# A hybrid decoder trunk on one core: transposes and bonus sums moved from TensorE to VectorE and DRAM trips

## Chip, core, metric

One core of a Trainium2 chip (trn2). The metric is the device time of one launch in microseconds, as the median of runs; lower is better. Matmuls run on TensorE, elementwise work on VectorE, ScalarE and GpSimd, and the DMA queues of SyncE (SP), ScalarE and GpSimd move data between DRAM and the on-chip memory.

## What is computed

Two pre-norm residual layers over 512 positions of width 1024. In each, one projection of the normed input feeds three branches, an RWKV-7 recurrence, a chunked retention and a chunked spatial gating unit; they are merged by sigmoid gates, and a gated MLP with a short causal convolution follows. The parts that the change touches, cut from the reference:

```python
def rwkv7_branch(p, mu, w0, w_up, a0, a_up, g_up, k_k, k_a, r_k, lnx_g, lnx_b):
    ...
    r, k, v, decay, a, kk = map(heads, (r, k, v, decay, a, kk))     # 8 heads of 64
    y = rwkv7_scan(r, decay, k, v, kk, a)
    mean = jnp.mean(y, axis=-1, keepdims=True)
    var = jnp.mean(jnp.square(y - mean), axis=-1, keepdims=True)
    y = (y - mean) * lax.rsqrt(var + RW_GN_EPS) * lnx_g + lnx_b
    y = y + jnp.sum(r * k * r_k, axis=-1, keepdims=True) * v        # the bonus
    return (y.reshape(B, S, RW_WIDTH) * g).astype(p.dtype)

def retention_branch(p, cos, sin):                                   # 4 heads, chunks of 128
    q, k, v, g = jnp.split(p, ...)
    q = rotary(q, cos, sin); k = rotary(k, cos, sin) * (RET_QK_DIM ** -0.5)
    scores = jnp.einsum('bhnid,bhnjd->bhnij', qc, kc) * decay_in[:, None]
    inner = jnp.einsum('bhnij,bhnje->bhnie', scores, vc)
    ...
```

## The kernel before

Every float32 matrix is split into a rounded high part and the remainder (`split`, `part`), and a product is three matmuls (`mm3`, L151): high by low, high by high, low by high. A weight unit is 128 x 512, loaded by SP (`load`, L121), split by ScalarE (L134) and VectorE (L135), and used by 12 matmuls of 512 columns. `unit` keeps three raw units and two to five split ones ahead.

A scheduler orders each engine's instructions by a modelled timeline and by the order in which the program emits them; `keep_in_program_order` (`po`) holds single instructions to the emitted order, and `pin` does so for matmuls. Engines work through their queues in that order. Tile pools have a fixed number of buffers: `u` has 31 (`NU`), `r` (pool `rg`) has 16 (`NR`), `f` 39 (`NFP`); a tile that finds none free waits for the last user of another.

A layer runs in this order.

- `rwkv`: columns of the projection give k, r, v with features on the partitions (`col`, four tiles of 128 features each, in `kc`, `rc`, `Vf`). `prep(m)` makes decays and the small products per chunk of 64 positions. `bonus(m)` multiplies r, k and `r_k` (L556), splits the product, sums it over each head's 64 partitions by two matmuls with a block matrix of ones (`bonesR`, L559 and L560) and multiplies by v (L561). It reads v as `col` left it.
- Turns by DRAM: `vturn` and `bturn` transpose 32 x 32 blocks on VectorE, write the tile to DRAM (`trip`, L229) and read it back with blocks exchanged (`turn`, L592), all on SP's queue. Four `vturn` and four `bturn(m, 0)`, the b, k of chunks 0 to 3, are emitted ahead of the solve.
- `solve`: a triangular solve of 32 x 32 blocks, a chain of some 70 VectorE instructions (L747 to L761), then `FILL[0]` filler steps and two sets of small matmuls (z at L771 into `zs`, then L780).
- The recurrence: eight chunks, each with three short bursts of 64 x 64 matmuls (L632), with one filler step ahead of each burst. In it the returned b, k are copied to their place by ScalarE (L635 before the loop, L647 inside), the state `S` is updated by VectorE (L677 to L680), and after each odd chunk y of 128 positions is normed.
- Filler steps (`fillers`) are independent projections of 12 matmuls a step: 24 gate columns, then q, k, v, g of the retention (`ret_proj`), then two of the gating unit. Inside `ret_proj`, `rotate` applies the rotary tables, fetched by ScalarE's queue (L825) when chunks 0 and 2 come up. `FILL` is (solve, between the solve's two products, recurrence). What is left of the filler runs after the recurrence.
- The rest: `sgu_v` alternates with `rwkv_out`, which transposes the four y tiles on TensorE (L712), applies scale and bias while it leaves PSUM (L714), adds the bonus and multiplies by the gate. Then merges, `ret_heads` (16 TensorE transposes of q, k at L847, copied out at L849), retention rows, output projection, and the MLP.

Of the kernel before, what the change touches and what calls it, by code (L numbers as in the profile page):

```python
# [18 lines left out]
NC = 4  # L19
# [3 lines left out]
NU, NR, NFP = 31, 16, 39  # L23
FILL = (36, 2, 1)
SEQ = "0 H 0 S 0 U S U S 0 S 0 0 S 2 2 Y 0 0 2 1 2 1 2 1 2 1 2 1 2 1 1 1"
# [22 lines left out]
class Emit:  # L48
# [170 lines left out]

    def turned(self, o, T, t):  # L220

        self.nc.vector.transpose(T.rearrange("p (f j d) -> p j f d", j=4, d=32), t.rearrange("p (j f d) -> p j f d", j=4, d=32))
        d = self.trip(T)
        for f in range(4):
            self.nc.sync.dma_start(o[32 * f:32 * f + 32, :].rearrange("d (a x) -> d a x", a=4), d[:, f * 128:f * 128 + 128].rearrange("(a d) x -> d a x", d=32))

    def trip(self, t):
        d = self.dp.tile([128, 512], F32, name=self.nm("tr"))
        self.nc.sync.dma_start(d, t)  # L229
        return d  # L230
# [69 lines left out]
    def run(self):  # L300
        nc, tc, a, V = self.nc, self.tc, self.a, self.nc.vector
        self.con = self.cp.tile([128, NCC], F32, name="con")
        self.rst = self.cp.tile([128, 512], F32, name="rst")
        self.bonesR = self.cp.tile([128, 128], F32R, name="bonesR")
        self.ones = self.cp.tile([128, 128], F32R, name="ones")
# [49 lines left out]
    def mixer(self, l, nst):  # L355
        self.pool = None
        with self.tc.tile_pool(name=f"rw{l}", bufs=1) as rp:
            self.rwp = rp
            self.filler = self.fillers(l)
            st = self.rwkv(l, nst)  # L360
        for _ in self.filler:
            pass
        self.rp = self.tc.tile_pool(name=f"ff{l}", bufs=NFP)
        self.fp = self.rp.__enter__()
        self.gup, self.bs, self.ws = self.f(n="gup"), self.f((128, 4, 128), n="bs"), self.f((128, 4, 128), n="ws")
        with self.tc.high_priority():
# [12 lines left out]
        rows = iter([(None, 0, (0, 1)), (0, 1), (1, 2, (2,)), (2, 3, (3,)), (3, None)])  # L379
        for step in SEQ.split():  # L380
            if step == "S":
                ysg += self.ret_row(*next(rows))
            elif step == "H":
                self.ret_heads()
            elif step == "U":
                next(rest), next(rest)
            elif step == "Y":
                yret = self.ret_out()
            elif step == "0":
                mg.append(self.merge(l, 0, len(mg), yrw))  # L390
# [41 lines left out]
    def rwkv(self, l, nst):  # L432
# [56 lines left out]
        X, Y, BK, Vf, bv = [], [], [], [], []  # L489
        kc, rc = [], []  # L490

        def cols3(m):
            kc.append(col(4 + m))
            rc.append(col(m))
            Vf.append(col(8 + m))

        def prep(m):


            k, r, v = kc[m], rc[m], Vf[m]  # L500
            ms = slice(m * 128, m * 128 + 128)
# [52 lines left out]
        def bonus(m):  # L554
            kp, r, v = kc[m], rc[m], Vf[m]
            V.scalar_tensor_tensor(kp, r, self.p("rk", m), kp, op0=MUL, op1=MUL)  # L556
            kh, kl = self.split(kp, self.r)
            pbn = self.sm()
            po(T.matmul(pbn, self.bonesR, kl, start=True, stop=False))  # L559
            po(T.matmul(pbn, self.bonesR, kh, start=False, stop=True))  # L560
            V.tensor_tensor(kp, v, pbn, op=MUL)  # L561
            bv.append(kp)

        if l == 0:
            self.tc.keep_in_program_order(V.memset(self.rst[:, 0:512:64], 0.0))
            A.copy(self.bonesR, self.c("bones"))
        cols3(0)
# [26 lines left out]
        def vturn(m):  # L594
            t, o = self.r(n="vT"), self.r(n="Vt")
            V.transpose(t.rearrange("p (j c d) -> p c j d", j=2, d=32), Vf[m].rearrange("p (c j d) -> p c j d", j=2, d=32))
            turn(o, self.trip(t), lambda h: 1 - h)
            Vf[m] = o

        def bturn(m, g):  # L600
            t, o = self.r(n="bkT"), self.r(n="bkS")
            V.transpose(t.rearrange("p (q c d) -> p c q d", c=4, d=32), BK[m][:, 4 * g:4 * g + 4].rearrange("p c a (e d) -> p c (a e) d", d=32))
            d = self.trip(t)
# [6 lines left out]
        for m in range(4):  # L610
            vturn(m)
        for m in range(4):
            bturn(m, 0)

# [8 lines left out]
        self.pool = None  # L623
        self.solve(GB, n2)

# [15 lines left out]
        for c in range(8):  # L641
            if c % 2 == 0:
                y = self.r(n="y")
            if c:
                self.fill(FILL[2], True)
            if back:
                po(A.copy(*back.pop(0)))  # L647
            if c < 4:
                bturn(c, 1)
            P1 = self.sm((128, 2, 4, 64))  # L650
# [49 lines left out]
            V.tensor_tensor(h8(y), h8(y), rs.unsqueeze(2).to_broadcast([128, 8, 64]), op=MUL)  # L700
            yT.append(y)
        return yT, bv, gd

    def rwkv_out(self, l, yT, bv, gd):
# [3 lines left out]
        for m in range(4):  # L708
            ms = slice(m * 128, m * 128 + 128)
            pt = self.sm()  # L710
            for c in range(NC):
                self.tc.keep_in_program_order(T.transpose(pt[:, c * 128:c * 128 + 128], yT[c][:, ms], self.c("ident")))  # L712
# [8 lines left out]

    def solve(self, G, n2):

# [37 lines left out]
        V.transpose(TT.rearrange("p u t -> p t u"), TS)  # L761
# [25 lines left out]
    def ret_proj(self, l):  # L787
# [4 lines left out]
        for c, ps in enumerate(pss):  # L792
            A.activation(qs[c], ps, AF.Identity, scale=self.rsT[:, c:c + 1])
        yield
        rot, pss = self.rotate(l, qs), []
        del qs
# [19 lines left out]

    def rotate(self, l, qs):

        nc, V, a, po = self.nc, self.nc.vector, self.a, self.tc.keep_in_program_order
        for c in range(NC):  # L820
            s = qs.pop(0)
            if c % 2 == 0:
                tab = [self.u((128, 2, 256), n="tab") for _ in range(2)]
                for i in range(2):
                    nc.scalar.dma_start(tab[i], a["rot"][:, i, c:c + 2, :])  # L825
            src = s.rearrange("p (h e d) -> p h e d", e=2, d=32)
# [13 lines left out]
    def ret_heads(self):  # L840

        A, V, T, po = self.nc.scalar, self.nc.vector, self.nc.tensor, self.tc.keep_in_program_order
        self.qF, self.kF = [], []
        for j in range(4):
            pt = self.sm((128, 4, 128))
            for c in range(NC):
                po(T.transpose(pt[:, c, :], self.ro[c][:, j * 128:j * 128 + 128], self.c("ident")))  # L847
# [10 lines left out]
    def ret_row(self, read, score, gates=()):  # L858
# [12 lines left out]
        if read is not None:  # L871
# [4 lines left out]
            for j, h in hd if read else ():  # L876
                mm(h, j, self.qF[j][hv[h], read, :], self.Rc[hv[h], j, :])
        if score is not None:
            for j, h in hd:
                mm(h, 2 + j, self.kF[j][hv[h], score, :], self.qF[j][hv[h], score, :])  # L880
        if read is not None:
# [369 lines left out]
```

## Time and profile before

| | |
|---|---|
| Median of three runs | 1726.6 us (1726.36 to 1728.52) |
| Profiled execution | 1725.19 us, span 1723.5 us |
| Mean granted TensorE clock | 0.998 |
| Busy: TensorE, VectorE, ScalarE, GpSimd | 1709.1, 1147.1, 765.0, 145.7 us |
| HBM traffic | 181.6 MB read, 23.1 MB written, 119 GB/s |

Times in the profile count from the start of the span, for one execution. In a row of instruction groups stand line, engine, operation, out<-in, shapes and count, then busy time and mean length of one in ns, then idle time just before them with what ended it. In a row of the chain stand start, length and what. PE is TensorE, PEld its weight load, DVE VectorE, ACT ScalarE, POOL GpSimd; a q behind the name is the engine's queue. Layer 0's solve and recurrence lie at about 125 to 303 us, layer 1's at 984 to 1153.

### The profile page before, as it was taken

Reading aid. Unit: us, or ns where it says so; the run is one execution under the profiler, and the core shown is the slowest. Engines: PE = TensorE matmul, PEld = TensorE weight load, DVE = VectorE, ACT = ScalarE, POOL = GpSimd, SP = SyncE. Lnnn points to the kernel's source line nnn. Section 1 sums busy time; section 2 is a strip of 40 time slices with the busy share of each in tenths; the row PEclk is TensorE's granted clock in tenths of the full one; section 3 lists DMA queues with packets and bytes.
Section 4 is the critical chain, followed back from the end, with each engine's and each line's share of the span. In section 5 each row is a group of like instructions: output and inputs, shape, how many; then the busy total and the mean of one; then the engine's idle time right before and its main releaser. Section 6 shows DMA issues by size and latency. Waiting matters only on the chain.

```text
span 1723.5 us, 27518 instructions
## 1 busy us (share of the span) xinstructions
PE 1709.1 (99%) x10432; PEld 1405.3 (82%) x10432; DVE 1147.1 (67%) x1968; ACT 765.0 (44%) x1280; POOL 145.7 (8%) x163
## 2 busy tenths in 40 slices
PE   9999999999999999999999999999999999999997
PEld 7788777888888888888888887778888888888887
DVE  6887745568669777653377886455776787776433
ACT  6563533534255444333265634345333544443322
POOL 2121000003200000000021300000131000000000
PEclk9999999999999999999999999999999999999999
DMA  5236542415443322233332465433254333222332
GB/s 179 86 110 209 166 142 93 142 61 169 155 147 98 98 98 96 71 119 112 110 110 80 126 214 162 125 115 113 75 198 144 129 98 98 98 98 64 107 96 83
DMA packets 120804, 206.50 MB, mean 120 GB/s; under 512 B 15072, under 2 KB 29664, under 8 KB 120672
## 3 DMA queue, kind: packets, MB, share of 16 engines
q1 hardware_dynamic: 105824, 172.28, 31.6%
q10 hardware_dynamic: 10368, 17.78, 2.9%
q0 software_dynamic: 4480, 14.68, 2.6%
q8 instruction: 82, 1.34, 0.3%
q14 instruction: 50, 0.41, 0.1%
HBM read 181.62 MB, written 23.07 MB: 119 GB/s over the span
## 4 chain that ended last, share of the span: by engine, by line
PE 94%; DVE 3%; DMA 2%; issue 1%; ACT 0%; SPq 0%; ACTq 0%; DVEq 0%
PE acc L151 87%; PE sm L632 2%; DMA wr<-wall 1%; PE sm L868 1%; DVE wl L135 1%; PE sm L542 1%; DVE cs L756 1%; DVE TMP L754 0%; PE sm L973 0%; DMA tr<-bkT 0%; DMA bkS<-tr 0%; PE sm L151 0%; ACT wh L134 0%; DVE cs L761 0%; PE sm L505 0%
## 5 line engine op out<-in xcount | busy, mean ns | idle before, releaser
L151 PE MATMUL acc<-lo,sh 128*128 128x512 f32 x1108 | 432.1, 390 | 0.0
L151 PE MATMUL acc<-hi,sh 128*128 128x512 f32 x1108 | 431.4, 389 | 0.0
L151 PE MATMUL acc<-hi,sl 128*128 128x512 f32 x1108 | 430.4, 389 | 0.0
L134 ACT CAST sh<-wr 128x512 fp32r<-128x512 f32 (+1 forms) x389 | 236.3, 612 | 390.5 <-PE acc L151 293.3
L135 DVE TENSOR_TENSOR sl<-wr,sh 128x512 fp32r<-128x512 f32 (+1 forms) x389 | 261.4, 676 | 185.8 <-ACT sh L134 90.3
L151 PEld LDWEIGHTS acc<-lo,sh 128*128 128x128 f32 x1108 | 208.0, 188 | 44.2 <-issue 0.7
L151 PEld LDWEIGHTS acc<-hi,sl 128*128 128x128 f32 x1108 | 208.0, 188 | 43.5 <-issue 0.2
L151 PEld LDWEIGHTS acc<-hi,sh 128*128 128x128 f32 x1108 | 208.0, 188 | 42.6
L151 PE MATMUL acc<-lo,wh 128*128 128x512 f32 x588 | 231.7, 394 | 0.7 <-ACT wh L134 0.5
L151 PE MATMUL acc<-hi,wl 128*128 128x512 f32 x588 | 230.2, 392 | 1.4 <-DVE wl L135 1.4
L151 PE MATMUL acc<-hi,wh 128*128 128x512 f32 x588 | 229.2, 390 | 0.0
L135 DVE TENSOR_TENSOR wl<-wr,wh 128x512 fp32r<-128x512 f32 x195 | 138.0, 709 | 131.8 <-ACT wh L134 126.4
L151 PE MATMUL acc<-ah,sh 128*128 128x512 f32 (+1 forms) x748 | 219.5, 377 | 0.0
L134 ACT CAST wh<-wr 128x512 fp32r<-128x512 f32 x195 | 120.0, 619 | 208.1 <-PE acc L151 147.2
L151 PEld LDWEIGHTS acc<-ah,sh 128*128 128x128 f32 x748 | 137.6, 188 | 25.8
L151 PE MATMUL acc<-ah,sl 128*128 128x512 f32 (+1 forms) x374 | 140.8, 377 | 0.0
L151 PEld LDWEIGHTS acc<-hi,wl 128*128 128x128 f32 x588 | 110.4, 188 | 27.3 <-DVE wl L135 3.5
L151 PEld LDWEIGHTS acc<-lo,wh 128*128 128x128 f32 x588 | 110.4, 188 | 25.1 <-ACT wh L134 1.0
L151 PEld LDWEIGHTS acc<-hi,wh 128*128 128x128 f32 x588 | 110.4, 188 | 22.4 <-issue 0.2
L1024 DVE TENSOR_TENSOR fu<-acc,rsF 128x512 f32<-128x512 f32 x88 | 60.7, 690 | 70.3 <-PE acc L151 70.2
L1026 ACT ACTIVATE cv<-fu,pc 128x512 f32<-128x512 f32 x88 | 71.6, 816 | 41.3 <-DVE fu L1024 37.0
L151 PEld LDWEIGHTS acc<-ah,sl 128*128 128x128 f32 x374 | 70.4, 188 | 12.9
(300 smaller groups left out, 2078.4 us busy)
## 6 DMA issues: line engine op xcount, KB each, us to landing
wr<-wall SPq DMA_DIRECT2D x488, 256.0 KB, 2.6
wr<-wdn SPq DMA_DIRECT2D x80, 256.0 KB, 2.7
gd<-gth ACTq DMA_DIRECT2D x48, 256.0 KB, 3.0
gth<-gd POOLq DMA_DIRECT2D x48, 256.0 KB, 3.3
tr<-bkT SPq DMA_DIRECT2D x16, 256.0 KB, 3.0
bkS<-tr SPq DMA_DIRECT2D x128, 32.0 KB, 2.4
tr<-vT SPq DMA_DIRECT2D x8, 256.0 KB, 2.5
Vt<-tr SPq DMA_DIRECT2D x32, 64.0 KB, 2.4
```

Source lines behind the costliest of these rows:

```text
L134: self.kept(self.nc.scalar.copy(hi[:, :n], raw[:, :n]))
L135: self.kept(self.nc.vector.tensor_tensor(lo[:, :n], raw[:, :n], hi[:, :n], op=SUB))
L151: i = self.nc.tensor.matmul(*x, **y)
L542: i = T.matmul(pK[hv[1 - h], j, :], bk[hv[h], c, 1, :], x[hv[h], c, :], start=True, stop=True)
L632: po(T.matmul(o, l, r, start=start, stop=True, skip_group_check=True))
L756: V.tensor_tensor(TS[:, k + 1:, :c], TS[:, k + 1:, :c], tmp, op=ADD)
L868: po(T.matmul(X[h][:, i, :], lhsT, rhs, start=new[h], stop=stop, skip_group_check=True))
L1024: V.tensor_tensor(u, ps, self.rsF, op=MUL)
L1026: A.activation(t, u, AF.Identity, scale=self.p("cw2", j), bias=self.p("cb", j))
```

## The change

- Bonus: `bonus(m)` keeps only the product (L556). The sum over a head is a new `bsum(m)`: a VectorE transpose, a reduction over runs of 32, an exchange of the two halves of a head by four small ScalarE copies, an add, a transpose of the result spread over 32 columns, and the product with v. It is emitted at the start of chunks 2 to 5 of the recurrence. v's original tile is kept for it (`vn`), and `bonesR` goes.
- b, k: the four `bturn(m, 0)` move into `turns`, called by `solve` after its last VectorE step. `bturn(·, 1)` is emitted two a chunk in chunks 0 and 1 instead of one a chunk in 0 to 3; the copies back come two a chunk in chunks 2 and 3.
- y: each normed y tile is turned with `turned` (one VectorE block transpose, one write, four reads on SP); `rwkv_out` reads it with four ScalarE activations of 128 x 128 per output tile.
- q, k: each rotated tile goes through `turned` after the recurrence; `ret_heads` copies the returned tiles with ScalarE. Scores and reads index by chunk instead of by feature tile.
- Tables: `tabs` issues the first pair when q, k leave PSUM, one filler step ahead of `rotate`, and the second at chunk 1 instead of 2.
- `FILL[0]` goes from 36 to 38.

```diff
-FILL = (36, 2, 1)
+FILL = (38, 2, 1)
...
+        self.qk = []
+        for c in range(NC):
+            self.qk.append(self.f(n="qkT"))
+            self.turned(self.qk[c], self.f(n="qkt"), self.ro[c], self.nc.sync)
...
         def bonus(m):
-            kp, r, v = kc[m], rc[m], Vf[m]
-            V.scalar_tensor_tensor(kp, r, self.p("rk", m), kp, op0=MUL, op1=MUL)
-            kh, kl = self.split(kp, self.r)
-            pbn = self.sm()
-            po(T.matmul(pbn, self.bonesR, kl, start=True, stop=False))
-            po(T.matmul(pbn, self.bonesR, kh, start=False, stop=True))
-            V.tensor_tensor(kp, v, pbn, op=MUL)
+            V.scalar_tensor_tensor(kc[m], rc[m], self.p("rk", m), kc[m], op0=MUL, op1=MUL)
+
+        def bsum(m):
+
+            kp, t = kc[m], self.rw((128, 2, 512), "cs", 3)[:, 0, :]
+            V.transpose(t, kp)
+            s, w = self.small((128, 16), "bs"), self.small((128, 16), "bw")
+            V.tensor_reduce(s, t.rearrange("p (j r) -> p j r", r=32), axis=AX.X, op=ADD)
+            for b in range(4):
+                A.copy(w[32 * b:32 * b + 32], s[32 * (b ^ 1):32 * (b ^ 1) + 32])
+            V.tensor_tensor(s, s, w, op=ADD)
+            V.transpose(kp, s.unsqueeze(2).to_broadcast([128, 16, 32]))
+            V.tensor_tensor(kp, vn[m], kp, op=MUL)
             bv.append(kp)
...
-        for m in range(4):
-            bturn(m, 0)
...
-        self.solve(GB, n2)
+
+        def turns():
+            for m in range(4):
+                bturn(m, 0)
+
+        self.solve(GB, n2, turns)
...
-            if back:
-                po(A.copy(*back.pop(0)))
-            if c < 4:
-                bturn(c, 1)
+            if 1 < c < 6:
+                bsum(c - 2)
+            for i in range(2):
+                if back and c > 1:
+                    po(A.copy(*back.pop(0)))
+                if c < 2:
+                    bturn(2 * c + i, 1)
...
-            yT.append(y)
+            o = self.r(n="yF")
+            self.turned(o, self.r(n="yt"), y, nc.sync)
+            yT.append(o)
...
-            pt = self.sm()
+            t = self.f(n="yF")
             for c in range(NC):
-                self.tc.keep_in_program_order(T.transpose(pt[:, c * 128:c * 128 + 128], yT[c][:, ms], self.c("ident")))
-            t = self.f(n="yF")
-            A.activation(t, pt, AF.Identity, scale=self.p("lg", m), bias=self.p("lb", m))
+                q = lambda x: x.rearrange("p (a d) -> p a d", d=32)
+                A.activation(q(t[:, 128 * c:128 * c + 128]), yT[c].rearrange("p (a j d) -> p a j d", j=4, d=32)[:, :, m, :], AF.Identity, scale=self.p("lg", m), bias=self.p("lb", m))
...
         diag(TT)
+        then()
...
+    def tabs(self, l, c):
+        t = [self.u((128, 2, 256), n="tab") for _ in range(2)]
+        for i in range(2):
+            self.nc.scalar.dma_start(t[i], self.a["rot"][:, i, c:c + 2, :])
+        return t
...
-            if c % 2 == 0:
-                tab = [self.u((128, 2, 256), n="tab") for _ in range(2)]
-                for i in range(2):
-                    nc.scalar.dma_start(tab[i], a["rot"][:, i, c:c + 2, :])
+            if c == 1:
+                tabs.append(self.tabs(l, 2))
+            tab = tabs[c // 2]
...
-        for j in range(4):
-            pt = self.sm((128, 4, 128))
-            for c in range(NC):
-                po(T.transpose(pt[:, c, :], self.ro[c][:, j * 128:j * 128 + 128], self.c("ident")))
-            t = self.r((128, 4, 128), n="qF" if j < 2 else "kF")
-            (V.tensor_copy if j % 2 else A.copy)(t, pt)
-            (self.qF if j < 2 else self.kF).append(t)
+        for c in range(NC):
+            t = self.r((128, 4, 4, 32), n="qF")
+            A.copy(t, self.qk[c].rearrange("p (a j d) -> p j a d", j=4, d=32))
+            t = t.rearrange("p j a d -> p j (a d)")
+            self.qF.append(t[:, 0:2])
+            self.kF.append(t[:, 2:4])
+        del self.qk
```

More of the change, by code (lines that the diff above doesn't have):

```diff
@@ L218, in norm_sq, with turned, trip @@
         st["acc"] = sq
-    def turned(self, o, T, t):
+    def turned(self, o, T, t, q):
         self.nc.vector.transpose(T.rearrange("p (f j d) -> p j f d", j=4, d=32), t.rearrange("p (j f d) -> p j f d", j=4, d=32))
-        d = self.trip(T)
+        d = self.trip(T, q)
         for f in range(4):
-            self.nc.sync.dma_start(o[32 * f:32 * f + 32, :].rearrange("d (a x) -> d a x", a=4), d[:, f * 128:f * 128 + 128].rearrange("(a d) x -> d a x", d=32))
-    def trip(self, t):
+            q.dma_start(o[32 * f:32 * f + 32, :].rearrange("d (a x) -> d a x", a=4), d[:, f * 128:f * 128 + 128].rearrange("(a d) x -> d a x", d=32))
+    def trip(self, t, q):
         d = self.dp.tile([128, 512], F32, name=self.nm("tr"))
-        self.nc.sync.dma_start(d, t)
+        q.dma_start(d, t)
         return d
@@ L303, in run @@
         self.rst = self.cp.tile([128, 512], F32, name="rst")
-        self.bonesR = self.cp.tile([128, 128], F32R, name="bonesR")
         self.ones = self.cp.tile([128, 128], F32R, name="ones")
@@ L489, in rwkv @@
         X, Y, BK, Vf, bv = [], [], [], [], []
-        kc, rc = [], []
+        kc, rc, vn = [], [], []
         def cols3(m):
@@ L495, in cols3 @@
             Vf.append(col(8 + m))
+            vn.append(Vf[m])
         def prep(m):
-            k, r, v = kc[m], rc[m], Vf[m]
+            k, r = kc[m], rc[m]
             ms = slice(m * 128, m * 128 + 128)
@@ L565, in rwkv @@
             self.tc.keep_in_program_order(V.memset(self.rst[:, 0:512:64], 0.0))
-            A.copy(self.bonesR, self.c("bones"))
         cols3(0)
@@ L596, in vturn @@
             V.transpose(t.rearrange("p (j c d) -> p c j d", j=2, d=32), Vf[m].rearrange("p (c j d) -> p c j d", j=2, d=32))
-            turn(o, self.trip(t), lambda h: 1 - h)
+            turn(o, self.trip(t, nc.sync), lambda h: 1 - h)
             Vf[m] = o
@@ L602, in bturn @@
             V.transpose(t.rearrange("p (q c d) -> p c q d", c=4, d=32), BK[m][:, 4 * g:4 * g + 4].rearrange("p c a (e d) -> p c (a e) d", d=32))
-            d = self.trip(t)
+            d = self.trip(t, nc.sync)
             for a in range(2):
@@ L720, in rwkv_out, with solve @@
             yield
-    def solve(self, G, n2):
+    def solve(self, G, n2, then):
         V, A, T = self.nc.vector, self.nc.scalar, self.nc.tensor
@@ L793, in ret_proj @@
             A.activation(qs[c], ps, AF.Identity, scale=self.rsT[:, c:c + 1])
+        tabs = [self.tabs(l, 0)]
         yield
-        rot, pss = self.rotate(l, qs), []
+        rot, pss = self.rotate(l, qs, tabs), []
         del qs
@@ L815, in ret_proj, with rotate @@
             yield
-    def rotate(self, l, qs):
+    def tabs(self, l, c):
[3 more added lines that the diff above has]
+        return t
+    def rotate(self, l, qs, tabs):
         nc, V, a, po = self.nc, self.nc.vector, self.a, self.tc.keep_in_program_order
@@ L840, in ret_heads @@
     def ret_heads(self):
-        A, V, T, po = self.nc.scalar, self.nc.vector, self.nc.tensor, self.tc.keep_in_program_order
+        A, V = self.nc.scalar, self.nc.vector
         self.qF, self.kF = [], []
-        for j in range(4):
-            pt = self.sm((128, 4, 128))
-            for c in range(NC):
-                po(T.transpose(pt[:, c, :], self.ro[c][:, j * 128:j * 128 + 128], self.c("ident")))
-            t = self.r((128, 4, 128), n="qF" if j < 2 else "kF")
-            (V.tensor_copy if j % 2 else A.copy)(t, pt)
-            (self.qF if j < 2 else self.kF).append(t)
+        for c in range(NC):
[5 more added lines that the diff above has]
+        del self.qk
         self.kd = []
@@ L876, in ret_row @@
             for j, h in hd if read else ():
-                mm(h, j, self.qF[j][hv[h], read, :], self.Rc[hv[h], j, :])
+                mm(h, j, self.qF[read][hv[h], j, :], self.Rc[hv[h], j, :])
         if score is not None:
             for j, h in hd:
-                mm(h, 2 + j, self.kF[j][hv[h], score, :], self.qF[j][hv[h], score, :])
+                mm(h, 2 + j, self.kF[score][hv[h], j, :], self.qF[score][hv[h], j, :])
         if read is not None:
```

## The prediction

> **What bounds the kernel now.** I read the page first, then the chain of waits in order of time, then the groups of instructions of TensorE, then the waits of TensorE alone.
>
> ```profile
> span 1723.5 us, 27518 instructions
> PE 1709.1 (99%) x10432; PEld 1405.3 (82%) x10432; DVE 1147.1 (67%) x1968; ACT 765.0 (44%) x1280; POOL 145.7 (8%) x163
> PE 94%; DVE 3%; DMA 2%; issue 1%; ACT 0%; SPq 0%; ACTq 0%; DVEq 0%
> 513.62 355.24 PE acc L151 x1567
> ```
>
> TensorE is busy in 99% of the span and makes 94% of the chain. A busy PE need not be a full one, so the last row, from the chain of waits in order of time, matters more: 1567 matmuls of 512 columns in 355.24 us is 0.2267 us each, back to back, for a fifth of the run. In such a kernel time comes from two places only: work that TensorE no longer does, and moments in which it stands. The waits of TensorE alone give the second; the rows that the change touches are these three.
>
> ```profile
> PE acc L151 <- DVE wl L135: 1.4, 2, 0.9
> PE sm L632 <- DVE s L691: 1.2, 2, 1.0
> PE sm L559 <- ACT Y L547: 0.8, 1, 0.8
> ```
>
> They hold 3.4 us (total, number, longest); the rest of TensorE's waits lie at the start and in the last rows of the output. So VectorE at 67%, ScalarE at 44% and the queues have room on average, and what must be asked is whether they have it where the change loads them.
>
> **What TensorE is rid of.** Three groups go entirely. Counts come from the groups by line, prices from the chain of waits, where a group stands with its real pitch (the groups' own mean is a pipelined length and would overstate it).
>
> ```profile
> L559 PE MATMUL sm<-lo,bonesR 128*128 128x512 f32 x8 | 3.3, 408 | 0.8 <-ACT Y L547 0.8
> L712 PE MATMUL sm<-con,y 128*128 128x128 f32 x32 | 4.8, 272 | 0.0
> L847 PE MATMUL sm<-con,ro 128*128 128x128 f32 x32 | 3.8, 272 | 0.0
> 88.78 0.24 PE sm L559
> 89.02 0.23 PE sm L560
> 347.57 0.44 PE sm L712 x4
> 373.03 1.75 PE sm L847 x16
> ```
>
> Bonus sums: eight pairs (L559, L560) of 0.24 + 0.23 us, 3.8 us. The read-out's transposes: 32 in groups of four at 0.44, 3.5 us. The q, k transposes: two groups of 16 at 1.75, 3.5 us. Together 10.8 us, nothing of which has other TensorE work beside it. FILL only moves filler steps from behind the recurrence to the solve; it adds no matmul.
>
> A transpose costs TensorE 0.11 us by these rows (1.75 over 16). [...]
>
> **Waits that go.** The bonus wait (0.8) goes with its matmul. The recurrence's wait (1.2) has its cause in VectorE's order of work:
>
> ```profile
> 273.04 0.82 ACTq L825 DMA_DIRECT2D tab<-rot  x2
> 277.50 0.69 DVE L831 TENSOR_TENSOR ro<-qs,tab 128x512 f32<-128x512 f32 x1 [3.12 <-DMA tab<-rot]
> 281.04 0.41 DVE L680 TENSOR_TENSOR S<-S,F 128x256 f32<-128x256 f32 x1
> 281.60 0.69 PE L632 MATMUL sm<-S,X 64*64 64x64 f32 x32 [1.01 <-DVE s L691]
> ```
>
> The rotation sat 3.12 us at the head of VectorE's queue for its tables, and the state's update L680 behind it came late for TensorE. Tables issued a filler step (12 matmuls, 2.7 us) and more earlier cover most of that: 1.2. The third (1.4, for a weight split at L135) falls at the end of the solve, where VectorE runs transposes of 2 us; VectorE gets 4 transposes and the last bonus split and product (4 x 0.70 + 1.4 = 4.2 us, rows below) out of its way there, and TensorE's weights four trips out of theirs on SP: 1.4. Waits together: 3.4. The best case is 10.8 + 3.4 = 14.2 us.
>
> **What is added, and what hides it.** Each layer gets eight block transposes (q, k and y), four bonus sums (two transposes, a reduction, a small add, a product), and eight trips through DRAM on SP (a 256 KB write, four 64 KB reads).
>
> ```profile
> L602 DVE STREAM_TRANSPOSE bkT<-bk 128x512 f32<-128x512 f32 x16 | 11.3, 704 | 0.1
> L536 DVE TENSOR_REDUCE pr<-cs 128x16 f32<-128x512 f32 x8 | 5.4, 677 | 0.0
> L144 DVE TENSOR_TENSOR lo<-rwc,hi 128x512 fp32r<-128x512 f32 x10 | 6.9, 685 | 0.6 <-ACT hi L143 0.6
> L619 DVE TENSOR_TENSOR n<-pr,sw 32x32 f32<-32x32 f32 x8 | 1.4, 176 | 0.2
> 228.00:239.00 11.00, 11.00 (x165) 8.62 (x164) 7.00 (x14) 5.38 (x10) 0.26 (x1) 1.00 0.49 147
> 272.00:284.00 12.00, 10.99 (x165) 8.47 (x164) 7.16 (x16) 5.18 (x10) 0.00 (x0) 1.00 0.37 115
> 303.00:347.00 44.00, 44.00 (x200) 36.38 (x196) 25.07 (x43) 23.97 (x41) 1.94 (x1) 1.00 0.46 144
> ```
>
> (The last three are stretches: length, PE, PEld, VectorE, ScalarE, GpSimd, clock, DMA share, GB/s.) q, k and the last y are turned in the 44 us before the read-out, where VectorE is busy 25 of 44 and the DMA engines 46%: four trips and four transposes fit, nothing on the path. ScalarE's sixteen small activations a layer instead of four large ones lie in the same slack. The bonus sum is 0.70 + 0.68 + 0.2 + 0.70 + 0.69, 3.0 us of VectorE in each of four chunks of the recurrence; a chunk lasts 11 us and holds 7 us of VectorE at its worst. So 10 of 11: it fits in throughput, but the state's update has only the 12 filler matmuls (2.7 us) before TensorE asks for it. I charge half of one 0.70 us operation as mean waiting, 0.35 us, in four chunks of each layer: 2.8 us in all. Its ends are 0 (the ordering puts the update first) and 0.7 in seven chunks of each layer, 9.8.
>
> The largest unknown is the four trips of b, k: they leave the solve and now start at its end, with the recurrence's first chunk as deadline, and the copies back on ScalarE (L635) stand before it. On SP's queue, weights, later trips and the reads all stand behind a read that waits for its write.
>
> ```profile
> 142.57 0.43 SPq L229 DMA_DIRECT2D tr<-bkT  x1
> 168.46 0.43 SPq L229 DMA_DIRECT2D tr<-bkT  x1
> 174.84 0.90 SPq L592 DMA_DIRECT2D bkS<-tr  x2
> L592 SPq DMA_DIRECT2D bkS<-tr x128: 303/426/2196, 146.1 to 1105.2; - x128
> bkS<-tr SPq DMA_DIRECT2D x128, 32.0 KB, 2.4
> tr<-bkT SPq DMA_DIRECT2D x16, 256.0 KB, 3.0
> 148.58 0.36 SPq L121 DMA_DIRECT2D wr<-wall  x1
> L635 ACT COPY bk<-bkS 128x512 f32<-128x512 f32 x8 | 4.4, 614 | 0.0
> L775 DVE COPY zs<-sm 32x256 f32<-32x256 f32 x8 | 3.4, 427 | 0.2
> 188.63 2.07 DVE cs L761
> 199.57 1.27 PE sm L771 x83
> 217.12 1.09 PE sm L632 x64
> 1045.47 2.01 DVE cs L761
> 1050.65 1.27 PE sm L771 x83
> 1068.23 1.09 PE sm L632 x64
> ```
>
> In layer 0 the first write of before went out at 142.57 and the last reads were issued by 175.7, 33.2 us for four trips one after another (fourth write at 168.46, 25.9 after the first); with 2.4 to land, 35.6 us. The solve ends at 190.7 there and, 4.2 earlier, at 186.5; the first write leaves 0.7 later. The chunk's burst that reads b, k stands at 217.1; two filler steps (24 x 0.2267 = 5.4) less one bonus pair (0.5) and one wait (0.6) put it at 221.4. Layer 1: writes from 1044.0, burst at 1068.2 + 5.4 - 0.5 - 0.8 = 1072.3. I take the trips as overlapping, since VectorE, idle at that point, can turn the next block while the first write is under way: 32 reads of 0.43 are 13.8 us, some weights of 0.4 between them 3 us, and 3.0 + 2.4 + 0.6 for first write, last landing and copy: 23 us, done at 210 and 1067, before both bursts. Cost nought; the other end is the next part.
>
> **The sum.** The profiled execution took 1725.2 us, its span and 1.7 around it; the median of the runs is 1726.6, 1.4 above. 1725.2 - 10.8 - 3.4 + 2.8 = 1713.8 for a profiled execution, 1715.2 as a median: 11.4 us or 0.66% faster.
>
> **The rivals.** One: the trips of b, k stay one after another. Then they are in place (0.6 for the last copy, L635) at 187.2 + 35.6 + 0.6 = 223.4 in layer 0, 2.0 after the burst, and at 1044.0 + 36.2 = 1080.2 in layer 1, 7.9 after: 9.9 us of TensorE, 1725.1. For it: SP issued them so before, each write after the previous trip's reads. Against: there VectorE was full of the solve, and there was no hurry.
>
> Two: VectorE becomes late in every chunk of the recurrence. Bonus sums, the y turn, rotations that now start two filler steps sooner and the splits meet; at the 9.8 end the time is 1726.6 - 14.2 + 9.8 = 1722.2. For it: the wait of 1.2 above came of one blocked instruction. Against: 7 busy us in the fullest chunk.
>
> Three, slower: the 16 buffers of the pool `rg` run out. v's original must now live until its bonus sum, so 13 are held through the solve (four each of k, v, turned v, and the gate), and three are left for four returned b, k blocks and the solve's two `zs`, which before had room for all. If `zs` gets its buffers only after the third copy back, with trips one after another, then it comes (two copies of L775 a pair, 0.8) at 187.2 + 25.9 + 2.4 + 0.6 + 0.8 = 216.9 in layer 0 and 1073.7 in layer 1. TensorE would want it after z and 24 fillers: 199.57 + 4.3 + 1.3 + 5.4 = 210.6 and 1061.5. It stands 6.3 + 12.2 = 18.5 us: 1733.7. It decides the sign when these waits pass 11.4 us over both layers. For it: the count of buffers. Against: overlapping trips free buffers sooner, and nothing prevents a copy back from running ahead of `zs`.
>
> **How the numbers follow.** A measurement of this kernel tells about 0.2% (3.5 us) from no change. Forecast 0.62; trips in series 0.14; VectorE late 0.12; buffers 0.12. The forecast's own range is 1711 to 1719: the best case is 1712.4, a microsecond more if hidden gaps go with the removed groups, and above it the charge of 2.8 doubled with a part of a late trip. The first rival can end anywhere between overlap and series; its half up to 1723 and three quarters of the second count as faster: 0.62 + 0.07 + 0.09 = 0.78. The other half of the first and the rest of the second are no change, 0.10; the third is slower, 0.12. The range up to 1723 leaves out the third rival and half of the first, 0.19.
>
> **What would show it.** Right: the three groups' work gone from PE; the pitch of L151 unchanged; PE's wait for the state's update gone from the chunk where rotations begin, and the `tab` wait of VectorE under 1 us; the last `bkS` landing ahead of the first chunk's burst. Wrong: a wait of TensorE at the first burst for `bk` (rival one), at the second solve product for `zs` (three), or before `S` in most chunks (two), of over 2 us in a layer. The forecast falls if PE's waits in the two recurrences exceed 8 us, or if the matmul pitch rises while the DMA share grows.

## The result: 1747.6 us, 1.2% slower

The changed kernel takes 1747.61 us (median of 4 runs, 1745.03 to 1749.05) against 1727.13 us for the kernel before, run beside it, a ratio of 1.012 with a 95% interval of [1.0105, 1.0135]. The prediction said 1715.2 us, with a range up to 1723. The profiled execution took 1747.07 us.

The first lines are from the page of the changed kernel (span, engines, shares of the chain), the last from its chain of waits in order of time (start, length, what).

```profile
span 1745.3 us, 27559 instructions
PE 1709.6 (98%) x10352; PEld 1400.6 (80%) x10352; DVE 1164.9 (67%) x2004; ACT 774.1 (44%) x1331; POOL 149.4 (9%) x163
PE 85%; DMA 7%; SPq 3%; DVE 2%; issue 1%; ACT 1%; ACTq 0%; POOL 0%; DVEq 0%; POOLq 0%
524.31 355.19 PE acc L151 x1567
```

TensorE issues 80 instructions fewer (16 bonus matmuls, 64 transposes) and the pitch in the undisturbed MLP is the same: 355.19 us for 1567. But the chain now runs through DMA and SP for 10%, where it was 2%. The page's busy shares hide the loss: VectorE stands at 67% and ScalarE at 44% in both kernels. TensorE's own waits show it (total, number, longest).

```profile
PE sm L644 <- DVE XB L669: 8.7, 5, 1.9
PE sm L644 <- ACT U L683: 5.6, 4, 2.2
PE acc L151 <- DVE wl L135: 3.6, 3, 2.4
PE acc L151 <- DVE sl L135: 2.5, 3, 1.8
PE acc L151 <- DVE cs L762: 2.3, 1, 2.3
```

They hold 22.7 us; the three rows of before held 3.4. The two relays of the recurrence, `XB` and `U`, had no row before. Next come windows of the changed kernel (length; busy times of TensorE, its weight load, VectorE, ScalarE, GpSimd; granted clock, DMA share, GB/s), the middle two being 3.9 us that begin 1.1 to 1.6 us behind the end of a stall.

```profile
117.00:121.00 4.00, 4.00 (x20) 3.30 (x19) 0.57 (x2) 1.30 (x3) 0.00 (x0) 1.00 0.63 173
125.50:129.40 3.90, 3.90 (x43) 2.86 (x45) 3.90 (x8) 2.00 (x7) 0.00 (x0) 0.57 0.56 203
234.70:238.60 3.90, 3.90 (x12) 2.87 (x10) 1.02 (x3) 0.66 (x2) 0.00 (x0) 0.56 0.64 202
200.00:300.00 100.00, 93.16 (x1343) 72.64 (x1342) 52.20 (x102) 39.28 (x79) 3.28 (x2) 0.98 0.45 138
```

TensorE is busy 93.16 of the 100 us that hold most of the first recurrence, and behind some stalls its granted clock also falls (0.56 or 0.57 over a window of 3.9 us, in which matmuls of 512 columns follow one another at 0.43 us, against 0.23 elsewhere). That happens four times; 4 x 3.9 x 0.43 is 6.7 us. The account of one execution: 21.8 us longer in span, and 10.8 us of work gone, so 32.6 to find. New waits give 19.3 from the rows shown, the slow clock 6.7. Of the other 6.6 about 2 are idle time outside these rows (TensorE stands 35.7 us in all, 14.4 before); the rest is busy time, and neither is attributed.

**What VectorE and ScalarE stood for.** VectorE's timeline in the changed kernel (start, length; the bracket holds the idle time just before and its cause), then two of its waits in total.

```profile
97.58 0.70 DVE L605 STREAM_TRANSPOSE vT<-rwc 128x512 f32<-128x512 f32 x1
112.21 0.71 DVE L611 STREAM_TRANSPOSE bkT<-bk 128x512 f32<-128x512 f32 x1 [3.80 <-DMA tr<-vT]
120.52 0.71 DVE L611 STREAM_TRANSPOSE bkT<-bk 128x512 f32<-128x512 f32 x1 [3.43 <-DMA tr<-bkT]
128.65 0.70 DVE L611 STREAM_TRANSPOSE bkT<-bk 128x512 f32<-128x512 f32 x1
198.78 0.70 DVE L611 STREAM_TRANSPOSE bkT<-bk 128x512 f32<-128x512 f32 x1
DVE bkT L611 <- DMA tr<-bkT: 10.4, 3, 4.4
DVE bkT L611 <- DMA tr<-vT: 3.8, 1, 3.8
```

The same turns in the kernel before, first v, first and last b, k of this group:

```profile
123.28 0.70 DVE L596 STREAM_TRANSPOSE vT<-rwc 128x512 f32<-128x512 f32 x1
138.25 0.71 DVE L602 STREAM_TRANSPOSE bkT<-bk 128x512 f32<-128x512 f32 x1
159.38 0.70 DVE L602 STREAM_TRANSPOSE bkT<-bk 128x512 f32<-128x512 f32 x1
```

"Behind the solve" held only in the text of the program: three of the four turns now run ahead of the solve, 23 to 26 us earlier than before, in the middle of `prep`, and the fourth 39 us later, behind it. There VectorE stands twice at the head of its queue, each time until an earlier turned tile has been written and its buffer is free; TensorE's stall of 2.4 us from 121.6 follows. None of these waits exists in the kernel before.

The bonus sums did not run where the program has them either. These are the first and the last VectorE step of the four sums, and TensorE's first burst of the recurrence, all in layer 0:

```profile
191.30 0.70 DVE L564 STREAM_TRANSPOSE cs<-rwc 128x512 f32<-128x512 f32 x1
206.98 0.69 DVE L571 TENSOR_TENSOR rwc<-rwc,rwc 128x512 f32<-128x512 f32 x1
221.86 0.51 PE L644 MATMUL sm<-Vt,Y 64*64 64x64 f32 x10
```

Emitted in chunks 2 to 5, they run right behind the solve, before the recurrence begins; in layer 1 it is the same (1049.2 to 1066.8, first burst at 1083.8).

ScalarE's waits in the changed kernel, and two lines of its timeline:

```profile
ACT bk L662 <- DMA bkS<-tr: 21.3, 6, 4.6
ACT wh L134 <- DMA yF<-tr: 4.9, 1, 4.9
ACT wh L134 <- DMA tab<-rot: 4.8, 1, 4.8
ACT bk L662 <- DMA tr<-bkT: 4.8, 2, 3.1
232.53 0.62 ACT L662 COPY bk<-bkS 128x512 f32<-128x512 f32 x1 [4.57 <-DMA bkS<-tr]
233.17 0.37 ACT L683 COPY U<-sm 128x256 f32<-128x256 f32 x1
```

and in the kernel before:

```profile
ACT bk L647 <- DMA bkS<-tr: 4.2, 3, 1.9
ACT bk L647 <- DMA tr<-bkT: 1.2, 2, 0.6
```

The copies of the returned b, k blocks (L662) stand in ScalarE's queue 26.1 us, before 5.4. Behind each lie weight casts (L134) and the recurrence's `U`: at 233.17 `U` follows a copy that waited 4.57 us for its reads, and TensorE stood 2.2 us for it.

The two single waits of 4.9 and 4.8 us are the earlier tables. In layer 0:

```profile
287.59 0.33 ACTq L838 DMA_DIRECT2D tab<-rot  x1
288.02 1.14 ACT L134 CAST wh<-wr 128x512 fp32r<-128x512 f32 x2 [4.90 <-DMA yF<-tr]
```

ScalarE's queue stands at the issue of the last table, by the profile until the reads of a y tile have landed, with a weight cast behind it, and TensorE then stands 1.9 us for `XB`; in layer 1 the same costs TensorE 1.8 us, with a granted clock of 0.56 behind it (1152.9 to 1156.8). With the tables alone (`e1_tabs`) there is no such wait. What the issue needs of y's reads is not shown.

### The profile page after: what moved, and what is told of

It reads as the page before. It is cut to its first block, busy times and chain, and to the rows that moved or that the text cites. A ratio compares the mean times of both kernels' runs of the same rounds, so it can differ in the third digit from the quotient of the medians.

```text
span 1745.3 us, 27559 instructions
## 1 busy us (share of the span) xinstructions
PE 1709.6 (98%) x10352; PEld 1400.6 (80%) x10352; DVE 1164.9 (67%) x2004; ACT 774.1 (44%) x1331; POOL 149.4 (9%) x163
## 4 chain that ended last, share of the span: by engine, by line
PE 85%; DMA 7%; SPq 3%; DVE 2%; issue 1%; ACT 1%; ACTq 0%; POOL 0%; DVEq 0%; POOLq 0%
PE acc L151 81%; SPq L601 2%; DMA wr<-wall 2%; DMA tr<-bkT 1%; PE sm L644 1%; DMA bkS<-tr 1%; PE sm L891 1%; DMA tr<-vT 1%; DVE wl L135 1%; ACT wh L134 0%; PE sm L996 0%; DMA tr<-qkt 0%; DMA x<-xT 0%; SPq L121 0%; DMA ws<-sgw 0%
## 5 line engine op out<-in xcount | busy, mean ns | idle before, releaser
L134 ACT CAST sh<-wr 128x512 fp32r<-128x512 f32 (+1 forms) x389 | 236.6, 612 | 407.7 <-PE acc L151 307.7
L134 ACT CAST wh<-wr 128x512 fp32r<-128x512 f32 x195 | 119.8, 619 | 202.7 <-PE acc L151 148.3
L151 PEld LDWEIGHTS acc<-hi,wh 128*128 128x128 f32 x588 | 111.5, 190 | 22.7 <-issue 0.3
```

The source lines that it names most:

```text
L134: self.kept(self.nc.scalar.copy(hi[:, :n], raw[:, :n]))
L151: i = self.nc.tensor.matmul(*x, **y)
```

## Experiments

All ratios are against the kernel before on the same chip, with 95% intervals; gains and losses in us are differences of medians. The edits are shown in excerpts.

**The four parts alone.** Each kernel is the one before with one part of the diff.

```diff
e1_tabs   +        tabs = [self.tabs(l, 0)]          # and the second pair at c == 1
e2_qk     +            self.turned(self.qk[c], self.f(n="qkt"), self.ro[c], self.nc.sync)
          -                po(T.transpose(pt[:, c, :], self.ro[c][...], self.c("ident")))
e3_yturn  +            self.turned(o, self.r(n="yt"), y, nc.sync)
          -                ...T.transpose(pt[...], yT[c][:, ms], self.c("ident"))
e4_rw     # bonus by bsum, turns() in solve, two turns a chunk, FILL[0] = 38
```

> The kernel before with the earlier rotary tables alone. Both theories: one wait of VectorE for the tables (3.1 us twice) shrinks, TensorE's wait of 1.2 us behind it goes, 1725.9 us (-1.2). If the tables, issued earlier on ScalarE's queue, stand there for a free buffer, ScalarE stops for up to 4.5 us a layer: up to 1731.

Measured 1725.61, ratio 0.9996 [0.9988, 1.0005]: no difference to be told.

> The kernel before with the q, k turns alone (TensorE loses 3.5 us of transposes, SP gets four trips a layer after the recurrence). Theory queue (weights stand on SP behind reads that wait for their own write): the waits that the changed kernel shows there, 3.2 us over both layers, come back, so 1726.8 us (no change). Theory buffers (only the 16 buffers of rg, filled by the kept v tiles, cause the loss): nothing is held here, -3.5, 1723.6 us.

Measured 1721.14, ratio 0.9968 [0.9956, 0.9979]: 5.2 us faster. This is the one part that pays, and the fastest kernel of this study, though why it gains more than it was priced at stays open. The interval is 3.6 to 7.6 us; the work removed was priced at 3.5.

> The kernel before with the y turns alone (TensorE loses 3.5 us of transposes, SP gets four trips a layer in and after the recurrence). Theory queue: weights late after each trip, some 8 us of waits and half clock as in the changed kernel, 1731 us (+4.5). Theory buffers: no v tile is kept, -3.5, 1723.6 us.

Measured 1737.21, ratio 1.0064 [1.0052, 1.0077]: 10.9 us slower, though it takes as much work from TensorE as the part before.

> The kernel before with the recurrence's part alone: bonus sums by VectorE, v kept, b, k behind the solve, two turns a chunk, FILL 38; q, k and y by TensorE as before. Theory queue: the remainder of the loss, 1746 us (+19). Theory buffers: here lies all of it and more, since the other parts gain 8 us, 1756 us (+29).

Measured 1741.56, ratio 1.0089 [1.0075, 1.0103]: 15.2 us slower. The four parts add up to -0.7 - 5.2 + 10.9 + 15.2 = +20.2 us, the whole loss (20.5). So there are two losses to explain, in the y turn and in the last part. That the four add up does not make them independent: other combinations below do not.

**The y turn.** Its waits of ScalarE and TensorE, and ScalarE's timeline, when it is made alone:

```profile
ACT bk L647 <- DMA bkS<-tr: 20.5, 3, 9.7
ACT bk L647 <- DMA tr<-bkT: 9.1, 1, 9.1
PE sm L632 <- ACT U L668: 7.8, 2, 4.2
257.12 0.62 ACT L647 COPY bk<-bkS 128x512 f32<-128x512 f32 x1 [9.66 <-DMA bkS<-tr]
257.64 0.61 ACT L134 CAST wh<-wr 128x512 fp32r<-128x512 f32 x1
258.16 0.36 ACT L668 COPY U<-sm 128x256 f32<-128x256 f32 x1
```

It costs by way of something that it does not touch: the third turn of b, k, at 235.7 before, comes at 241.6, behind the y turn, and ScalarE stands 9.66 us at the copy of its return, with a weight cast and `U` behind it. For its profiled execution, 15.9 us longer in span and 3.5 of work gone make 19.4; waits for `U` and `XB` give 11.2. The granted clock was 0.83 over 254 to 264 us and 0.66 over 267 to 277. Its mean over the execution was 0.994, against 0.998 before, by which I estimate up to some 7 us (0.006 x 1739.4 less 0.002 x 1723.5); at least 1 is left. Two edits test the cause: copy the returned blocks on GpSimd, so that nothing of TensorE's stands behind them; or take y's trip off SP's queue.

```diff
f1_yturn_pc (e3_yturn with)
-                po(A.copy(*back.pop(0)))
+                po(nc.gpsimd.tensor_copy(*back.pop(0)))
h1_yturn_q (e3_yturn with)
-            self.turned(o, self.r(n="yt"), y, nc.sync)
+            self.turned(o, self.r(n="yt"), y, nc.gpsimd)
```

> The y turns alone, and the copies of returned b, k done by GpSimd instead of ScalarE. In the y turns alone ScalarE stood 9.7 and 6.3 us at such a copy, with weight casts and the copy of U behind it. Theory ScalarE (that stand is the loss): 7.8 + 3.4 us of TensorE's waits and some 3 us of half clock go, 1737 - 14 = 1723 us. Theory SP (raw weights late on SP behind the reads): the casts come no sooner, 1735 us or more.

Measured 1728.34, ratio 1.0015 [1.0005, 1.0024]: 2.4 us slower in place of 10.9. TensorE's wait for `U` is gone; what is left is mainly the wait for the copies themselves:

```profile
PE sm L632 <- POOL bk L647: 4.7, 2, 3.0
```

> The y turns alone, their trips on GpSimd's queue instead of SP's; copies of b, k on ScalarE as before. Theory SP order (the y trip stands ahead of the b, k trip and so makes ScalarE stand at the copy): b, k trips as in the kernel before, the 3.5 us of transposes gained, 1723 us. If the y turn costs by something else (VectorE, ScalarE's small activations): 1735 us or more.

Measured 1737.10, ratio 1.0058 [1.0043, 1.0073], as on SP. The third and fourth turn of b, k come no sooner (243.8 and 247.7), so it is not SP's queue that holds them. On VectorE the third again stands right behind the turn of y (243.2 and 243.8; on SP 241.0 and 241.6).

**The bonus and the b, k turns apart.**

```diff
f3_bkmove   # before, with turns() in solve, two turns a chunk, FILL[0] = 38
f4_bonus    # before, with bonus/bsum of the diff, v kept in vn
g1_hold     # before, with v kept as f4_bonus keeps it, the sums as before
+            if 1 < c < 6:
+                V.tensor_copy(self.rw((128, 2, 512), "cs", 3)[:, 0, 0:1], vn[c - 2][:, 0:1])
g2_bonus_early  # before, with bonus by VectorE, but within prep, so v isn't kept
+            bsum(m)
```

> The kernel before with b, k behind the solve, two turns a chunk and FILL 38 alone; bonus sums by TensorE, so no v tile is kept. Theory buffers for the part ahead of the solve (VectorE stands at a block transpose for one of 16 buffers): no such stand here; with trips in time 1724 us, with copies late on ScalarE in the recurrence up to 1734 us.

Measured 1725.81, ratio 0.9998 [0.9989, 1.0008]. VectorE's timeline has the first and the last of these turns where they were before (138.25 and 159.38):

```profile
138.40 0.70 DVE L602 STREAM_TRANSPOSE bkT<-bk 128x512 f32<-128x512 f32 x1
158.72 0.70 DVE L602 STREAM_TRANSPOSE bkT<-bk 128x512 f32<-128x512 f32 x1
```

The move behind the solve moved nothing. The second group, now two a chunk, did move (207.3 to 230.4, before 202.7 to 244.7), at no cost that can be told.

> The kernel before with the bonus sums by VectorE alone, v kept, b, k turned ahead of the solve as before. Theory buffers: 13 of 16 are held and four returned b, k blocks want room, VectorE stands for buffers ahead of the solve and at the end of it; 3.8 us less TensorE work, 10 us or more of waits: 1733 us or more. If buffers don't matter: 1722 us.

Measured 1744.92, ratio 1.0104 [1.008, 1.0128]: 18.9 us slower. The bonus alone has more than the whole loss of the fourth part, and the waits that mark it, of VectorE and of ScalarE:

```profile
DVE bkT L607 <- DMA tr<-bkT: 10.9, 3, 4.2
DVE bkT L607 <- DMA tr<-vT: 3.4, 1, 3.4
ACT bk L654 <- DMA bkS<-tr: 25.6, 6, 5.5
```

> The kernel before, nothing taken away and nothing moved: only one column of each v tile is copied by VectorE in a buffer that comes free after the solve, so that four buffers of rg stay taken as long as in the changed kernel. Theory buffers: VectorE stands at block transposes of b, k for 10 us or more ahead of the solve as in the bonus part alone, and the loss of that run comes back without its 3.8 us of gain: 1740 us or more. Theory VectorE load (the bonus sum's instructions are the loss): no change, 1726 us.

Measured 1728.96, ratio 1.002 [1.0011, 1.0029]: 2.4 us slower, not the 14 or more that the theory of buffers expected. With v kept (nearly as long as in `f4_bonus`: its copies run at 192.7 to 195.5, the sums there until 209.2) and the sums left on TensorE, VectorE does stand for buffers, but v's turns begin at 123.9 as before, and ScalarE's copies wait 4.0 us in all, less than before:

```profile
DVE bkT L603 <- DMA tr<-bkT: 8.6, 2, 4.8
```

In `f4_bonus` they begin at 97.7. The difference between the two kernels is that `f4_bonus` no longer splits the product into two `rg` tiles and no longer sums on TensorE, so room in the pool would come earlier, and v's turns, then b, k's, move up into `prep`; and that VectorE makes the sums behind the solve. Keeping v alone is a small part of the price. How the rest divides between the earlier turns and the sums' place was not tested, so the way by way of freed buffers is argued, not shown.

> The kernel before with the bonus sums by VectorE where the matmuls stood, so that v is not kept. Theory buffers: the 3.8 us of matmuls and the bonus wait are gained, 1722 us. Theory VectorE load: 1.6 us more in each of four preps, in a stretch where VectorE is busy 31 of 37 us, comes back as late weight splits: 1727 us or more.

Measured 1732.98, ratio 1.0041 [1.0026, 1.0056]: 6.4 us slower. With the sums in `prep` the waits for buffers are gone, but TensorE waits for `prep`'s own products:

```profile
PE sm L504 <- ACT GB L546: 2.6, 2, 2.4
PE sm L504 <- ACT Y L547: 1.6, 2, 1.2
```

In neither place was the bonus on VectorE worth its 3.8 us on TensorE.

**Cures for the changed kernel.**

```diff
f2_after_pc          # after, copies of b, k by GpSimd (as f1)
g3_after_early_pc    # f2, and bsum(m) within prep
g4_qk_early          # before, with tables, q, k turns and bsum(m) within prep
h2_qky_q             # before, with tables, q, k turns, y turns on GpSimd's queue
h3_nr20              # after, with
-NU, NR, NFP = 31, 16, 39
+NU, NR, NFP = 27, 20, 39
h4_nr20_pc_yq        # h3, copies by GpSimd, y trips on GpSimd's queue
```

> The changed kernel with the copies of returned b, k done by GpSimd. Theory ScalarE: the waits in both recurrences before U and XB (14 us) and half of the half-clock time go, 1747 - 18 = 1729 us; what stays is ahead of the solve (7 us) and at the read-out. Theory SP: 1745 us.

Measured 1733.23, ratio 1.0043 [1.0027, 1.0058]. Against 1.012 this gives back 13 us of 20.5 by moving copies that are 0.6 us each: some two thirds of the loss goes when ScalarE no longer stands at them.

> The changed kernel with bonus sums in prep (v not kept) and the copies of returned b, k on GpSimd. If buffers and ScalarE's stand are the two causes, nearly the whole forecast gain appears: 10.8 us of matmuls less some 4 us of late trips of y and q, k on SP, 1719 us. If there is a third cause, over 1726 us.

Measured 1738.24, ratio 1.0074 [1.0059, 1.0089]: with the sums in `prep` the changed kernel is 4.4 us worse than with the copies' cure alone. By the expectation's own words there is a third cause; `g2_bonus_early`, 6.4 us slower alone, points to VectorE's sums in `prep`.

> The kernel before with the parts that are not expected to cost: q, k turns, earlier tables, bonus sums in prep; y and b, k as before. Sum of the parts: -5.2 (measured for q, k) - 3.8 - 0.7: 1716 us. Theory VectorE load: 1721 us.

Measured 1732.32, ratio 1.0038 [1.0024, 1.0053]. The sum of its parts would be +0.5 us; it is +5.8, so here the parts are not independent.

> q, k turns on SP, y turns on GpSimd's queue, earlier tables; bonus and b, k as before. Theory SP order: -5.2 (q, k, measured) - 3.5 - 0.7, 1717 us. Otherwise 1730 us or more.

Measured 1732.50, ratio 1.0038 [1.0023, 1.0052], +6.3 us; the sum of its parts is +5.0.

> The changed kernel with 20 buffers in rg and 27 in u instead of 16 and 31. Theory buffers: VectorE no longer stands at the b, k transposes (14 us of stand now), the fourth trip needs not wait for a v tile, and 10 us or more come back: 1737 us or less. If buffers only follow: 1747 us; four fewer u buffers may cost some of it.

Measured 1760.28, ratio 1.0192 [1.0173, 1.0211]: more buffers made it worse. VectorE no longer stands for buffers at its b, k turns in this trace; all four now run in `prep` (108.3 to 129.0), and ScalarE stands 5 us ahead of one of `prep`'s copies, by the profile until a read of b, k has landed:

```profile
133.39 0.59 ACT L551 COPY Y<-sm 128x512 f32<-128x512 f32 x1 [5.01 <-DMA bkS<-tr]
```

TensorE stands 4.1 us there. So the full pool was not only a cause of stalls; it seems also to have been the brake that kept trips out of `prep`. The run does not separate this from the four `u` buffers that it gives up, which may cost time of their own.

> The changed kernel with 20 buffers in rg, copies of b, k on GpSimd and y trips on GpSimd's queue. If these three causes are the loss: the forecast's time with q, k's waits, 1717 to 1721 us. If the trips and transposes in the midst of prep cost by themselves: 1730 us.

Measured 1751.23, ratio 1.0142 [1.0126, 1.0157]. No cure of the whole beats the kernel before.

**The y turn after the recurrence.** One theory was left for y: that it costs by its place, between the turns of b, k.

```diff
i1_ylate (before with)
+        for y in yT:
+            ys.append(self.f(n="yS"))
+            self.turned(ys[-1], self.f(n="yt"), y, nc.sync)     # start of rwkv_out
i2_qk_ylate    # the same, and the q, k turns of e2_qk
```

> The kernel before with the read-out's turn by VectorE and DRAM, but made after the recurrence, in the block of the mixer that turns q and k in the kernel after: y stays in rg as before, and its turned copies take buffers of the mixer's pool of 39. What it tells apart: in the run of the y turns alone (1737.2) the third and fourth turn of b, k came 6 to 8 us late and ScalarE then stood 16 us at their copies. Theory A, the y turns cost because their four extra rg tiles and their place in the recurrence push those turns back: then without them 3.5 us of TensorE's transposes go and nothing comes in, 1721 to 1724. Rival B, the y turns cost because of what they themselves wait for (eight 4-byte-strided reads on SP ahead of the read-out, behind the weights): then the wait only moves, the read-out's first group stands for the trips of four tiles, some 8 to 10 us a layer, 1730 to 1745. Rival C, the trip is hidden but VectorE's and ScalarE's share in the mixer makes up for it: 1726, no change.

Measured 1735.92, ratio 1.0061 [1.0048, 1.0075]: theory A fell, rival B holds. (The reads are sixteen a layer, four for each of four tiles, of rows of 128 floats; not eight with a stride of 4 bytes.) Waits of ScalarE and TensorE, and SP's timeline:

```profile
ACT yF L718 <- DMA yS<-tr: 11.2, 4, 3.7
PE sm L151 <- DVE yF L722: 5.5, 2, 2.7
350.56 1.73 SPq L225 DMA_DIRECT2D yS<-tr  x4
352.38 0.38 SPq L229 DMA_DIRECT2D tr<-yt  x1
354.49 1.73 SPq L225 DMA_DIRECT2D yS<-tr  x4
356.31 0.38 SPq L229 DMA_DIRECT2D tr<-yt  x1
358.41 1.73 SPq L225 DMA_DIRECT2D yS<-tr  x4
```

The trips go in series at 3.9 us each, reads of one before the write of the next; the last reads go out at 360.1, and the read-out's first group, which needs all four tiles, stands for them. The third and fourth turn of b, k are back where they were before (235.9 and 244.9), so in the recurrence it was the turn of y that pushed them; behind it the y trips are late themselves. Either way it is some 10 us.

> The same late turn of y, with the q, k turns of the kernel after beside it. By theory A the two gains add: 1726.3 less 5.2 (q, k alone) less 3 to 4, 1716 to 1719, below any version so far. By rival B the y trips stand behind the four q, k trips on SP's queue, and the sum is 1725 to 1740. By rival C 1721, the gain of q, k alone.

Measured 1738.41, ratio 1.0073 [1.0061, 1.0086]: the gain of the q, k turns does not add to it. Eight trips now follow one another on SP ahead of the read-out.

## Why the prediction was wrong, point by point

- **What TensorE is rid of (10.8 us): right.** The groups are gone and the pitch is unchanged. For q, k, where nothing else came in its way, the gain was 5.2 us, more than the 3.5 priced.
- **Waits that go (3.4): the smaller part held.** The bonus wait went, and the wait for the state fell from 1.2 to 0.4. But the tables alone brought no time that can be told, VectorE's wait for them was still 1.6 us at its longest, not under 1, and in the whole change ScalarE stood nearly 5 us a layer at their issue, which no term had. The third, for a weight split, was sized from work that would leave the solve's end; that work was never there to leave, and such waits rose from 1.4 to 3.6 and 2.5.
- **The b, k trips start after the solve and overlap (cost nought): the step that failed first.** I took the place in the program for the place in time. The order on VectorE is the scheduler's, and the diff holds no instruction to its place here. Alone the move changed nothing. The last read did land at 209.8, near the 210 forecast and ahead of the first burst, but only because three of the four trips had been made long before; that agreement is luck. The rows quoted should have warned me: before the change these turns, emitted ahead of the solve, ran inside it (writes from 142.57 to 168.46).
- **Bonus in the recurrence (2.8, at most 9.8): the same mistake, and the term most mis-sized.** I charged VectorE's time in four chunks; the sums ran between the solve and the first chunk, and no row shows TensorE waiting for them. Alone, the bonus cost 18.9 us net, so some 23 us with the 3.8 of TensorE counted. Its trace shows that as VectorE standing for buffers in `prep` and ScalarE standing at copies in the recurrence, which a sum of busy times can't show; what in the bonus sets this off is only argued above.
- **"Nothing on the path" for q, k and y: right for q, k, wrong for y.** The step priced four trips and a share of busy time over 44 us. It left out that three of the four y turns lie in the recurrence, where VectorE takes the first of them ahead of b, k's third, and who stands behind a late return: ScalarE's copy, and behind it casts and `U`. The price was 10.9 us instead of nought.
- **Rival three had the right shortage in the wrong place.** It named `rg`, but let `zs` wait; TensorE has no row that waits for `zs`. The waits arose earlier, on VectorE in `prep`, and later, on ScalarE in the recurrence. Its 1733.7 was 14 us short, and its chance was put at 0.12.
- **Rival two's wait for `S` did not come** (0.4 us in the changed kernel); the waits stand before `XB` and `U` instead, 14.3 us in the two recurrences, past the 8 us that the prediction named as its end.
- **The slow clock behind a stall** was in no term: 6.7 us.
- **Transposes off TensorE.** Of the two sets moved, one move paid (5.2 us faster) and one did not (10.9 us slower). What decided was not the price of the transpose on either engine (1.75 us for 16 on TensorE, 0.70 us for VectorE's turn of a 128 x 512 tile) but who waits for the trip by DRAM that follows VectorE's turn of 32 by 32 blocks in this kernel.

What stays open: why q, k gave 5.2 us, what in the bonus moves the turns up, and 6.6 us of the changed kernel's loss.

## What to carry to other kernels

In this kernel, where TensorE is busy 99% of the time, work moved off it paid where its consumer held up nothing that TensorE needed (q, k: 5.2 us faster) and cost time where it did (y: 10.9 us slower). So before pricing the new work, list for each new DMA which in-order queue holds the instruction that waits for it, and what stands behind that one. A step emitted later under a scheduler is not thereby run later; look in the trace at what releases it, and count each pool's buffers over time, since a buffer freed early may pull work forward into a fuller stage, as it seems to have done here. When a part of a change can be had alone, measure it alone: here one of four parts gained 0.3%, and two others lost 1.5%.

## What the runs showed of the hardware

Idle times of TensorE of 1.8 to 2.4 us were followed by a granted clock of 0.56 to 0.57 over windows of 3.9 us, at four places in the changed kernel (from 125.5, 234.7, 995.9 and 1152.9); others of 1.9 and 1.8 us (from 288.5 and 350.8) were followed by 1.00 (290.4 to 294.3 and 352.6 to 356.5). By the windows shown such a stall cost 1.7 us more than itself (3.9 x 0.43). The length of the pause alone does not tell the two apart: one of 1.79 us (to 1152.05) stands among the first, one of 1.92 us (to 290.43) among the others. What does was not shown.
